# Moving the weight-sum transfers and the residual arithmetic of the MLP within a two-layer DiT kernel

## The chip, the cores and the metric

One core of one Trainium2 chip runs the whole program. The metric is the device time in microseconds (us) from the start to the end of one execution, lower being better. A measurement of this kernel can tell a change of about half a per cent.

## What is computed

The reference is a two-layer transformer block over 1024 latent tokens and 256 context tokens of width 1024, in fp32. Cut to what matters here:

```python
for l in range(2):                                       # need_ctx only for l == 0
    m_lat = silu(c) @ mod_w[l] + mod_b[l]                # shifts, scales, gates; m_ctx alike
    h  = modulate(xl, sh1, sc1)
    yl = mixer(h)      # l=0: Hyena long convolution + neighbourhood attention (natten)
                       # l=1: latent attention (MLA) + Fourier mixing
    xl = layer_norm(ALPHA * xl + g1 * yl)
    xl = layer_norm(ALPHA * xl + g2 * mlp(modulate(xl, sh2, sc2), mlp_w1[l], mlp_w2[l]))
    # the same two lines for xc where need_ctx
mlp(h, w1, w2) = square(relu(h @ w1)) @ w2               # 1024 -> 4096 -> 1024
```

## The kernel before, in words

Every fp32 product is made of three matrix products of rounded high and low parts (`mm3`, lines 168 to 170): ScalarE (ACT) makes the high part with a cast (L161), VectorE (DVE) the low part with a subtraction (L162), TensorE (PE) multiplies. The order of work on each engine is fixed when the program is built. DMAs are issued from two queues: SyncE (SP) issues the plain loads and stores, GpSimd (POOL) issues the others, and a queue that waits for one transfer's condition holds everything behind it. POOL also does small arithmetic: products of the convolution (L1030 to L1034, `sc`, `xc`), attention biases (L862, `n_g`), copies (`ob`), and reciprocal roots (L177, L194, L1838).

The stages, with their place in the profiled execution:

- **First stage** (0 to about 570 us, `first_stage`, L716): 24 blocks of input projections (`hyena_in`, `qkv_in`; raw weights `hwr`, split weights `hwh` and `hwl`, result `u`), woven with the spectra of the Hyena filters (`filter_spectra`; tiles `f_w`, `f_w3h`, `f_h`, `f_sdh`, `f_z`, `f_cf`, stored as `cfl`) and with modulation vectors (`modraw`, `modacc`).
- **Attention and convolution** of layer 0 (570 to 940 us, `attention_and_conv`): 80 jobs of neighbourhood attention, each with a row sum `acc`, woven with the long convolution.
- **Output projection** of layer 0 (940 to 1085 us, `mixer_out`).
- **MLP of layer 0** (`FastMlp`). The two products of the MLP are done with a seven-product scheme in place of eight (`PRODUCTS`, L1339). The first product is done in `pairs` (1085 to 1400 us): 16 pairs j, each with seven items; the partial sums for the first six (`EARLY`) were done ahead, during `mixer_out`, and their results wait in DRAM as `first` and `sums`. The item named `five` loads them back: `after5` (L1609) issues the loads of `m_e` from `first` (L1612) and `m_c` from `sums` (L1613) on SP behind the five-product, and then makes `m_f = m_y - m_e` (L1615), for which the next product's bank waits.
- **Context** (1400 to 1500 us, `context`, layer 0 only), then **passes** (1500 to 1910 us, `passes`, L1707): seven passes i = 0 to 6 over the hidden width, one product each, accumulating in 4 or 5 PSUM banks (m is the block of 128 rows). A bank is opened at i = 0, 2 and 4 (`OPENS`), and after the last item of a pass each bank is evicted (`evict`, L1761) by ACT or DVE into the 512-wide halves of the accumulators `m_ra` and `m_rb` (one for each half of the tokens). After i = 4 `close` and after i = 5 `base` (L1853, L1863) do the residual over the whole 1024 columns: `residual_sum` (L1818) loads the old x as `mres` on POOL (L1822), multiplies the accumulator by the gate (L1823), adds ALPHA times x (L1825); then come the statistics (`bn_stats`) and the normalisation (`norm`). `tail` (L1869) does this for the last 512 columns after i = 6.
- **Layer 1** repeats it: `MixerIn` and `mixer_cd_in` (1850 to 2065 us; `cx` loads, `c_pt` transposes, Fourier tables `d_csh` and `d_csl`), `mla` (2065 to 2480 us), `mixer_out`, pairs (2600 to 2720 and on), passes to 3237.5 us.

Small pieces of such vector work are queued in `self.side` and `self.late`, and each item of the MLP takes one or two from it (`aside(n)`, L1810).

Four of the right-hand factors of the second product (t1 to t4) are sums of blocks of `mlp_w2`. They are made by DMA alone: `weight_sums` (L1344) issues, per layer, 64 transfers of 512 KB on POOL into DRAM tiles `tsums`, plain copies and accumulating ones; and ahead of the four chains' first copies a 1x1 transfer (L1353) that reads a tile of the stage (`k.token`), to tie the transfers to the progress of the work. For each of eight tiles i the eight transfers follow one another, each on the result of the one before. Layer 0's are all taken in the first stage, four per block from block 5 on; layer 1's in `mla`, two per group of scores.

Of the kernel before, what the change touches and what calls it, by code (L numbers as in the profile page):

```python
# [10 lines left out]
F32 = mybir.dt.float32  # L11
F32R = mybir.dt.float32r
AF = mybir.ActivationFunctionType
ALU = mybir.AluOpType
# [213 lines left out]
def setup(k, es):  # L228
# [12 lines left out]
    k.silu = c.tile([128, KT, 2], F32, name="silu")  # L241
    k.co = {(s, t): c.tile([128, 2], F32, name=f"co{s}_{t}") for s in range(2) for t in range(NTT)}
# [438 lines left out]
def hyena_in(k, j, hw, up, pj):  # L681
# [4 lines left out]
    k.token = raw[0:1, 0, 0:1]  # L686
# [5 lines left out]
    for s, n in SPANS:  # L692
# [5 lines left out]
        else:  # L698
            nc.scalar.copy(u[:, L:], ps[:, :n])
    v = up.tile([128, T], F32, tag="uv", name="uv")  # L700
# [15 lines left out]
def first_stage(k, hp, er):  # L716
# [4 lines left out]
    with ExitStack() as es:  # L721
# [14 lines left out]
        sums = weight_sums(k, 0)  # L736
# [13 lines left out]
        for j in range(1, 24):  # L750
# [12 lines left out]
            for _ in range(4 if j > 4 else 0):  # L763
                next(sums, None)
# [22 lines left out]
def qkv_in(k, j, hw, up, pj):  # L787
# [7 lines left out]
    k.token = raw[0:1, 0, 0:1]  # L795
# [4 lines left out]
    for s, n in SPANS:  # L800
        yield
        ps = project(k, pj, wh, wl, s, n)
        nc.scalar.activation(out=u[:, s:s + n], in_=ps[:, :n], func=AF.Copy, scale=-0.125 if j < 4 else 1.0)
    yield
# [61 lines left out]
def natten(k, es, step):  # L866
# [89 lines left out]
    def attend(p, jobs):  # L956

        acc = sm.tile([128, 4, 2], F32, tag="acc", name="acc")[:, :len(jobs)]
        for ji, e in [(ji, e) for ji in range(len(jobs)) for e in range(2)]:
# [16 lines left out]
            lasts.append(vals)  # L976
            pend.append((p, e, job, ji, len(jobs), acc, pr))
# [366 lines left out]
def weight_sums(k, l):  # L1344

    w2 = k.mlp_w2[l].rearrange("(j t p) (d n) -> p j t d n", t=2, p=128, d=2)
    for i, dst in enumerate(k.tsums[l]):
        for to, term, add in ("t1", "b11", 0), ("t3", "b12", 0), ("t1", "b12", 1), ("t3", "b22", 1), ("t2", "t3", 0), ("t2", "b11", 1), ("t4", "t2", 0), ("t4", "b21", 1):  # L1350
# [3 lines left out]
            k.nc.gpsimd.dma_start(out=dst[:, RIGHT[to]], in_=src, accum_op=ALU.add if add else ALU.bypass)  # L1354
            yield True
# [32 lines left out]
class FastMlp:  # L1388
# [161 lines left out]
    def pairs(self):  # L1550

        k, nc, tt = self.k, self.k.nc, self.k.nc.vector.tensor_tensor
        new = lambda nm: self.out.tile([128, 512], F32, tag=nm, name="m_" + nm, bufs=2 if nm in "efgc" else 1)
# [6 lines left out]
        def item(p, make, bank, b, first, after):  # L1560
            def multiply(w):
                if first:
                    setattr(p, bank, self.bank(bank))
                self.product(getattr(p, bank), w, b, first)
# [9 lines left out]
        def pair(j):  # L1574
# [34 lines left out]
            def after5():  # L1609
                if early:  # L1610
                    p.e, p.c = new("e"), new("c")
                    nc.sync.dma_start(out=p.e, in_=k.first[j])  # L1612
                    nc.sync.dma_start(out=p.c, in_=k.sums[0, j // 2][:, j % 2])  # L1613
                p.f, p.g = new("f"), new("g")
# [901 lines left out]
```

## Time and profile before

| quantity | value |
|---|---|
| median of 3 runs | 3245.53 us (3235.15 to 3253.18) |
| the profiled execution's own time | 3239.32 us |
| its span, first to last instruction | 3237.5 us |
| TensorE busy (matmul) | 3055.5 us, 94% |
| VectorE, ScalarE, GpSimd busy | 2326.8, 1513.3, 534.6 us |
| mean granted TensorE clock | 0.977 |
| bytes moved by DMA | 557.82 MB, 172 GB/s |

The rows of the profile read as engine, tile names (written<-read) and line; a bracket at the end of a timeline row is the idle time of that engine just before the instruction, and what ended it. In rows by window there follow the window's length, each engine's busy time with its instructions in parentheses, the granted clock of TensorE, the share of the 16 DMA engines that were busy, and GB/s. In rows of waits: who waited, for whom, total us, times, longest. "SPq" is SyncE's issuing side. "PEld" is TensorE's loading of weights.

### The profile page before, as it was taken

What the parts mean: (1) busy time and instruction counts of PE and PEld (TensorE: products, weight loads), DVE (VectorE), ACT (ScalarE), POOL (GpSimd) and SP (SyncE); (2) the same over time, 40 slices, a digit from 0 to 9 for tenths busy, and PEclk for the clock granted to TensorE, in tenths of its full rate; (3) what the DMA queues carried; (4) which work ended last, traced back from release to release, by engine and by line L of the source; (5) the groups of instructions that cost most, each with busy time, mean ns of one, the idle gap of its engine ahead of it and who ended that gap; (6) DMA issues with size and microseconds to landing.
All of it is one profiled execution on the core that took longest, in us unless ns stands there. A gap on an engine that the chain in (4) does not pass through costs nothing. (4 is left out here: it accounts for less than half of the span.)

```text
span 3237.5 us, 46425 instructions
## 1 busy us (share of the span) xinstructions
PE 3055.5 (94%) x16500; PEld 2541.9 (79%) x16500; DVE 2326.8 (72%) x4456; ACT 1513.3 (47%) x3131; POOL 534.6 (17%) x800
## 2 busy tenths in 40 slices
PE   8898989899999899999999989999999999999997
PEld 4787878688877678888888777788888777888876
DVE  6566666788868876677675986688787887664577
ACT  3343333355553445555444445566665354554441
POOL 2202110222212121210000213112111212120000
PEclk9999999899999999999999999999999999999999
DMA  7648885433153464498785653255356355446564
GB/s 253 189 136 232 221 219 179 142 104 122 59 184 121 149 212 144 159 295 287 257 271 170 231 169 109 86 105 116 89 114 184 128 176 180 149 165 211 194 239 144
DMA packets 363557, 557.82 MB, mean 172 GB/s; under 512 B 33557, under 2 KB 226875, under 8 KB 362684
## 3 DMA queue, kind: packets, MB, share of 16 engines
q1 hardware_dynamic: 299484, 367.44, 35.2%
q0 software_dynamic: 63840, 187.41, 20.3%
q8 instruction: 130, 2.13, 0.3%
q14 instruction: 103, 0.84, 0.1%
HBM read 429.86 MB, written 193.65 MB: 193 GB/s over the span
## 5 line engine op out<-in xcount | busy, mean ns | idle before, releaser
L161 ACT CAST m_ph<-m_sl 128x512 fp32r<-128x512 f32 x216 | 134.1, 621 | 352.1 <-PE m_y L169 106.4
L162 DVE TENSOR_TENSOR m_pl<-m_sl,m_ph 128x512 fp32r<-128x512 f32 x216 | 148.5, 687 | 167.9 <-ACT m_ph L161 167.2
L161 ACT CAST m_ph<-m_w 128x512 fp32r<-128x512 f32 x224 | 135.9, 618 | 196.2 <-PE m_x L169 73.9
L315 DVE SCALAR_TENSOR_TENSOR modacc<-modraw,silu,modacc 128x512 f32<-128x512 f32 x224 | 162.5, 747 | 81.5 <-DMA modraw<-in_mod_w 80.6
L168 PE MATMUL pj<-hTh,hwh 128*128 128x512 f32 (+1 forms) x576 | 211.3, 368 | 1.4 <-ACT u L697 1.4
L169 PE MATMUL pj<-hTl,hwh 128*128 128x512 f32 (+1 forms) x576 | 209.2, 364 | 0.3 <-DVE hTl L219 0.3
L170 PE MATMUL pj<-hTh,hwl 128*128 128x512 f32 (+1 forms) x576 | 208.6, 362 | 0.3 <-DVE hwl L162 0.3
L162 DVE TENSOR_TENSOR m_pl<-m_w,m_ph 128x512 fp32r<-128x512 f32 x224 | 152.5, 683 | 9.8 <-ACT m_ph L161 9.4
L162 DVE TENSOR_TENSOR m_pl<-m_sr,m_ph 128x512 fp32r<-128x512 f32 x216 | 147.9, 685 | 6.7 <-ACT m_ph L161 4.6
L169 PE MATMUL m_x<-m_pl,m_ph 128*128 128x512 f32 x352 | 139.9, 398 | 6.1 <-DVE m_pl L162 6.1
L168 PE MATMUL m_x<-m_ph 128*128 128x512 f32 x352 | 131.6, 394 | 9.4 <-ACT m_ph L161 6.5
L170 PE MATMUL m_x<-m_ph,m_pl 128*128 128x512 f32 x352 | 138.8, 394 | 0.0
L161 ACT CAST m_ph<-m_sr 128x512 fp32r<-128x512 f32 x216 | 133.6, 619 | 9.1 <-PE m_x L169 5.9
L2341 ACT ACTIVATE a_p<-a_s,a_m 128x512 f32<-128x512 f32 (+1 forms) x192 | 116.3, 615 | 44.7 <-DVE a_m L2337 44.2
L1354 POOL DMA_DIRECT2D tsums<-in_mlp_w x96 | 96.8, 1021 | 220.6 <-DMA tsums<-tsums 108.2
L168 PEld LDWEIGHTS pj<-hTh,hwh 128*128 128x128 f32 x576 | 111.3, 194 | 18.6 <-ACT u L697 1.6
L169 PEld LDWEIGHTS pj<-hTl,hwh 128*128 128x128 f32 x576 | 111.6, 194 | 17.6 <-DVE hTl L219 1.6
L170 PEld LDWEIGHTS pj<-hTh,hwl 128*128 128x128 f32 x576 | 111.2, 193 | 17.2 <-DVE hwl L162 0.6
L2332 DVE TENSOR_REDUCE a_mx<-a_s 128x1 f32<-128x512 f32 (+1 forms) x192 | 110.9, 594 | 14.5 <-PE a_s L170 12.9
L168 PE MATMUL o_ps<-o_wh,yh 128*128 128x512 f32 x288 | 114.5, 400 | 2.1 <-ACT o_wh L161 2.1
L169 PE MATMUL o_ps<-o_wl,yh 128*128 128x512 f32 x288 | 114.3, 397 | 1.1 <-DVE o_wl L162 1.1
L170 PE MATMUL o_ps<-o_wh,yl 128*128 128x512 f32 x288 | 113.5, 395 | 0.0
(1319 smaller groups left out, 9928.8 us busy)
## 6 DMA issues: line engine op xcount, KB each, us to landing
m_sl<-sums SPq DMA_DIRECT2D x112, 512.0 KB
m_w<-in_mlp_w SPq DMA_DIRECT2D x108, 512.0 KB
tsums<-in_mlp_w POOLq DMA_DIRECT2D x96, 512.0 KB, 6.6
modraw<-in_mod_w SPq DMA_DIRECT2D x160, 256.0 KB
sums<-m_s POOLq DMA_DIRECT2D x128, 256.0 KB, 3.8
m_sr<-tsums SPq DMA_DIRECT2D x64, 512.0 KB
m_sr<-in_mlp_w SPq DMA_DIRECT2D x48, 512.0 KB
tsums<-tsums POOLq DMA_DIRECT2D x32, 512.0 KB, 4.0
```

The costliest lines, as they stand in the source:

```text
L161: nc.scalar.copy(hi, src)
L162: nc.vector.tensor_tensor(out=lo, in0=src, in1=hi, op=ALU.subtract)
L168: t.matmul(out, lh, rh, start=start, stop=False, skip_group_check=on)
L169: t.matmul(out, lh, rl, start=False, stop=False, skip_group_check=on)
L170: t.matmul(out, ll, rh, start=False, stop=stop, skip_group_check=on)
L315: k.nc.vector.scalar_tensor_tensor(out=acc, in0=w, scalar=c, in1=acc, op0=ALU.mult, op1=ALU.add)
L1354: k.nc.gpsimd.dma_start(out=dst[:, RIGHT[to]], in_=src, accum_op=ALU.add if add else ALU.bypass)
L2332: nc.vector.tensor_reduce(out=mx[:, i:i + 1], in_=ps[:, :n], axis=AX.X, op=ALU.min)
L2341: nc.scalar.activation(out=p_[:, s:s + n], in_=ss[i][:, :n], func=AF.Exp, bias=m, scale=-1.0, accum_out=acc[:, i:i + 1])
```

## The change

Four things are changed.

1. **Weight sums.** `weight_sums` goes through the eight terms outermost and the eight tiles innermost, so that a transfer's predecessor on the same tile lies eight transfers back. The 1x1 transfers are gone. In their place a POOL copy of one element (`k.after` from a token) stands before every transfer, and both are kept in program order. Layer 0: ACT copies one element of the block's result (`k.last`, a piece of `u`) into `k.tokens` in blocks 3 to 18, and two transfers follow in each of these blocks (32 in all); the other 32 are sent in attention, after jobs whose count leaves 1 or 3 modulo 5, with the job's `acc` as token. Layer 1: one transfer per score tile in `mla`, two per group as before.
2. **Early pairs.** The loads of `m_e` and `m_c` move from `after5` to `before5`, ahead of the five-product, and `m_e` has three buffers in place of two. Of the late sums, the last two change places.
3. **Passes.** The scaled input and the gate are applied to 512-wide partial sums: `base(m, half, h)` is queued after i = 1 (half 0, columns 0), i = 2 (half 1, columns 1) and i = 3 (the other two). What i = 4 and i = 5 bring is evicted as `q = ps * gate` (`gated`; 4 or 5 buffers `m_q`), and added to the accumulator later, with the statistics. `close` is then `end` and `norm`.
4. **Pacing.** The context takes a piece of side work at odd items alone; passes take one piece per item except in layer 0 outside i = 4 and outside odd items of i = 5, where they take two; the side work is emptied before the last item of i = 4.

The diff, cut:

```diff
+    for to, term, add in ("t1", "b11", 0), ("t3", "b12", 0), ("t1", "b12", 1), ("t3", "b22", 1), ("t2", "t3", 0), ("t2", "b11", 1), ("t4", "t2", 0), ("t4", "b21", 1):
+        for i, dst in enumerate(k.tsums[l]):
+            token = yield True
             src = dst[:, RIGHT[term]] if term in RIGHT else w2[...]
-            if not add and term not in RIGHT:
-                k.nc.gpsimd.dma_start(out=dst[0:1, RIGHT[to], 0, 0:1], in_=k.token)
-            k.nc.gpsimd.dma_start(out=dst[:, RIGHT[to]], in_=src, accum_op=ALU.add if add else ALU.bypass)
-            yield True
+            keep(nc.gpsimd.tensor_copy(k.after, token))
+            keep(nc.gpsimd.dma_start(out=dst[:, RIGHT[to]], in_=src, accum_op=ALU.add if add else ALU.bypass))
...
-            for _ in range(4 if j > 4 else 0):
-                next(sums, None)
+            if 2 < j < 19:
+                nc.scalar.copy(k.tokens[:, j:j + 1], k.last[0:1, 0:1])
+            for _ in range(2 if 2 < j < 19 else 0):
+                send(sums, k.tokens[:, j:j + 1])
...
+            if count[0] % 5 in (1, 3):
+                send(k.early_sums, acc[0:1, ji, e:e + 1])
...
-            def after5():
+            def before5():
                 if early:
                     p.e, p.c = new("e"), new("c")
                     nc.sync.dma_start(out=p.e, in_=k.first[j])
                     nc.sync.dma_start(out=p.c, in_=k.sums[0, j // 2][:, j % 2])
+
+            def after5():
                 p.f, p.g = new("f"), new("g")
                 tt(out=p.f, in0=p.y, in1=p.e, op=ALU.subtract)
...
+            elif i < 4:
+                tt(out=(b, a)[i - 2][:, hi], in0=ps, in1=b[:, lo], op=ALU.subtract)
             elif i < last:
-                d, x, y = ((b, ps, b[:, lo]), (a, ps, b[:, lo]), (a, a[:, hi], ps), (b, b[:, hi], ps))[i - 2]
-                tt(out=d[:, hi], in0=x, in1=y, op=ALU.subtract)
+                ends[m] = self.gated(self.tile_of(m, i - 4), (a, b)[i - 4], ps, hi, ALU.subtract, self.st[m, i - 4][:, 1])
+                next(ends[m])
...
+    def gated(self, t, a, ps, s, op, st):
+        tt = self.k.nc.vector.tensor_tensor
+        q = self.sm.tile([128, 512], F32, tag="q", name="m_q", bufs=5 if self.ctx else 4)
+        tt(out=q, in0=ps, in1=self.gate(t)[:, s], op=ALU.mult)
+        yield True
+        tt(out=a[:, s], in0=a[:, s], in1=q, op=op)
+        self.k.nc.vector.bn_stats(st, a[:, s])
+        yield True
...
-                self.aside(2)
+                self.aside(1 if not self.ctx or i == 4 or i == 5 and j % 2 else 2)
```

How the order of instructions moves on POOL, at three places. The first is the first stage, from the filter tables' loads on: `erp` and `rpx` are tables for the attention's biases, `tsums0_0` the sums' first tile. Before:

```order
L1353 DMA tsums0_0_233<-hwr_1805 1x1 x2
L1354 DMA tsums0_0_233<-in_mlp_w2 128x2x512 x4
L1354 DMA tsums0_0_233<-tsums0_0_233 128x1024
L666 DMA erp_256<-rp_zero_998 64x192
L667 DMA erp_256<-rp_zero_998 64x192
L1354 DMA tsums0_0_233<-in_mlp_w2 128x2x512
L671 DMA rpx_257<-erp_256 8x8x384 x16
```

The same place on POOL in the changed kernel:

```order
L668 DMA erp_258<-rp_zero_1000 64x192
L669 DMA erp_258<-rp_zero_1000 64x192
L673 DMA rpx_259<-erp_258 8x8x384 x16
L1361 COPY after_73<-tokens_74 1x1
L1362 DMA tsums0_0_235<-in_mlp_w2 128x2x512
```

The bias tables' transfers now stand ahead of every weight sum, and each weight sum has its copy of a token ahead of it.

The second place is attention on POOL, between two of the convolution's groups of products: `sc`, `xc` and `vc` are these products, `n_g0` a bias, `ob` an output of attention. Before:

```order
L1099 TENSOR_TENSOR vc_5630<-xc_5639 128x256
L862 TENSOR_TENSOR n_g0_5148<-n_g0_5148,rp_6545 128x256
L911 COPY ob_6128<-r_6126 128x512
L1030 TENSOR_TENSOR sc_6151<-xc_6152,cfc_5690 128x512
L1031 TENSOR_TENSOR xc_6152<-xc_6152,cfc_5690 128x512
```

The changed kernel has, from the same products on:

```order
L1105 TENSOR_TENSOR vc_5636<-xc_5645 128x256
L1106 TENSOR_TENSOR vc_5636<-xc_5645 128x256
L867 TENSOR_TENSOR n_g0_5150<-n_g0_5150,rp_6563 128x256
L1361 COPY after_73<-acc_5675 1x1
L1362 DMA tsums0_2_237<-tsums0_2_237 128x1024
```

Copies that wait for a job's `acc`, and transfers (this pair is the first of four that follow one another), now stand between the convolution's products; before, nothing of the sums was left in attention.

The third place is the boundary of the layers on POOL, where the last rows of layer 0 are stored (`xs1`) and layer 1's first work is prepared: `mres` is the old x, `cx` the new x read back. Before:

```order
L1822 DMA mres_18735<-xs0_6_129 128x1024
L1822 DMA mres_18753<-xs0_7_130 128x1024
L1822 DMA mres_18759<-xs0_9_132 128x1024
L2010 DMA cx_18865<-xs1_0_133 128x1024
L2010 DMA cx_19263<-xs1_1_134 128x1024
```

In the changed kernel all `mres` loads stand further ahead, `cx` follows its row's store at once, and the end of this part reads:

```order
L1864 DMA xs1_9_144<-m_rb4_13917 128x1024
L2108 DMA c_bdh_19784<-const_bdh 128x256
L2108 DMA c_bdl_19786<-const_bdl 128x256
L194 TENSOR_TENSOR co1_9_94<-co1_9_94,mhalf_65 128x1
L2199 DMA d_csh_19792<-const_csh 128x1024
L2260 COPY wqh_19736<-wqh_19736 128x3x8 x4
L2260 COPY wql_19737<-wql_19737 128x3x8 x4
L2199 DMA d_csl_19794<-const_csl 128x1024
L177 TENSOR_TENSOR rstd_19800<-rstd_19800,mhalf_65 128x1
```

The first loads of the Fourier tables `d_csh` and `d_csl` stood just ahead of the `mres` load of row 2 before; now they stand behind the last row's store, with reciprocal roots queued behind them.

More of the change, by code (lines that the diff above doesn't have):

```diff
@@ L699, in hyena_in @@
             nc.scalar.copy(u[:, L:], ps[:, :n])
+    k.last = u[:, L:]
     v = up.tile([128, T], F32, tag="uv", name="uv")
@@ L735, in first_stage @@
         extra = [(j, part) for j in range(2, 6) for part in range(2)]
-        sums = weight_sums(k, 0)
+        sums = k.early_sums = weight_sums(k, 0)
+        next(sums)
         steps = filter_spectra(k, tab, hid2, tneg, wk, ph, pz)
@@ L803, in qkv_in @@
         nc.scalar.activation(out=u[:, s:s + n], in_=ps[:, :n], func=AF.Copy, scale=-0.125 if j < 4 else 1.0)
+    k.last = u
     yield
@@ L1558, in store, with item @@
             nc.gpsimd.dma_start(out=k.sums[i, j // 2][:, j % 2], in_=a)
-        def item(p, make, bank, b, first, after):
+        def item(p, make, bank, b, first, after, before=lambda: None):
             def multiply(w):
@@ L1771, in run @@
             def run(*ops):
+                while i == 4 and j == nj - 1 and self.side:
+                    self.aside(1)
                 if i in OPENS and j == 0:
@@ L1816, in aside, with stats @@
                 self.side.pop(0)
-    def residual_sum(self, t, a):
-        nc = self.k.nc
-        x = self.xp.tile([128, D], F32, tag="mx", name="mres")
-        nc.gpsimd.dma_start(out=x, in_=self.src[t])
-        nc.vector.tensor_tensor(out=a, in0=a, in1=self.gate(t), op=ALU.mult)
-        yield True
-        nc.vector.scalar_tensor_tensor(out=a, in0=x, scalar=ALPHA, in1=a, op0=ALU.mult, op1=ALU.add)
-        yield True
-    def stats(self, m):
-        return self.sm.tile([128, 2, 6], F32, tag=f"st{m}", name="m_st")
+    def stats(self, m, half):
+        return self.sm.tile([128, 2, 6], F32, tag=f"st{m}{half}", name="m_st")
     def norm(self, t, a, st):
@@ L1851, in norm, with base, close @@
             yield True
-    def close(self, m, a):
-        t = self.tile_of(m, 0)
-        yield from self.residual_sum(t, a)
-        st = self.stats(m)
-        for h, s in enumerate(HALVES):
-            self.k.nc.vector.bn_stats(st[:, h], a[:, s])
-        yield True
-        yield from self.norm(t, a, st)
-    def base(self, m, a):
-        yield from self.residual_sum(self.tile_of(m, 1), a)
-        st = self.st[m] = self.stats(m)
-        self.k.nc.vector.bn_stats(st[:, 1], a[:, HALVES[1]])
+    def base(self, m, half, h):
+        nc = self.k.nc
+        t, s = self.tile_of(m, half), HALVES[h]
+        a = (self.ra, self.rb)[half][m][:, s]
+        x = self.xp.tile([128, D], F32, tag="mx", name="mres")[:, :512]
+        nc.gpsimd.dma_start(out=x, in_=self.src[t][:, s])
+        nc.vector.tensor_tensor(out=a, in0=a, in1=self.gate(t)[:, s], op=ALU.mult)
+        nc.vector.scalar_tensor_tensor(out=a, in0=x, scalar=ALPHA, in1=a, op0=ALU.mult, op1=ALU.add)
+        yield True
+        if half == h:
+            self.st[m, half] = self.stats(m, half)
+        if half == h == 0:
+            nc.vector.bn_stats(self.st[m, 0][:, 0], a)
+    def gated(self, t, a, ps, s, op, st):
[6 more added lines that the diff above has]
+        yield True
+    def close(self, m, end):
+        yield from end
+        yield from self.norm(self.tile_of(m, 0), self.ra[m], self.st[m, 0])
     def tail(self, m, ps):
-        a, s, tt = self.rb[m], HALVES[0], self.k.nc.vector.tensor_tensor
         while self.side:
@@ L1874, in tail @@
         t = self.tile_of(m, 1)
-        q = self.sm.tile([128, 512], F32, tag="q", name="m_q", bufs=2)
-        tt(out=q, in0=ps, in1=self.gate(t)[:, s], op=ALU.mult)
-        tt(out=a[:, s], in0=a[:, s], in1=q, op=ALU.add)
-        self.k.nc.vector.bn_stats(self.st[m][:, 0], a[:, s])
-        last = self.norm(t, a, self.st[m])
+        for _ in self.gated(t, self.rb[m], ps, HALVES[0], ALU.add, self.st[m, 1][:, 0]):
+            pass
+        last = self.norm(t, self.rb[m], self.st[m, 1])
         if self.then:
@@ L2390, in mla @@
         sums = weight_sums(k, 1)
+        next(sums)
         def advance():
@@ L2415, in mla @@
                     roped(g)
-                k.token = pr[0][1][0:1, 0:1]
-                for _ in range(2):
-                    next(sums, None)
+                for _, r in pr:
+                    send(sums, r[0:1, 0:1])
                 if g == 1 and h + 1 < NH:
```

30 lines of the change are left out of this document (19 added, 11 removed).

## The prediction

> **What bounds the kernel now.** I read the page's busy times and the granted clock first, then the busy times by stage, then the waits of TensorE and the timeline at its longest gaps.
>
> ```profile
> PE 3055.5 (94%) x16500; PEld 2541.9 (79%) x16500; DVE 2326.8 (72%) x4456; ACT 1513.3 (47%) x3131; POOL 534.6 (17%) x800
> core 0: 3237.5 us, clock 0.977
> ```
>
> TensorE is the bound: it is busy 3055.5 of 3237.5 us, so 182 us are idle. The clock is a second loss: a mean of 0.977 means that about 0.023 x 3237.5 = 74 us of full speed were not granted. The change adds no product and takes none away, so all that it can win lies in these 182 + 74 = 256 us. Where they lie, by stage (the columns after the length are PE, PEld, DVE, ACT, POOL, granted clock, DMA share, GB/s):
>
> ```profile
> 100.00:500.00 400.00, 363.22 (x2101) 318.73 (x2100) 255.57 (x500) 141.71 (x252) 76.23 (x98) 0.94 0.76 201
> 600.00:940.00 340.00, 325.03 (x2569) 274.14 (x2569) 273.48 (x587) 185.74 (x441) 65.77 (x74) 0.97 0.30 98
> 1050.00:1200.00 150.00, 132.46 (x541) 103.97 (x541) 114.17 (x183) 67.38 (x118) 32.47 (x58) 0.94 0.55 179
> 1200.00:1400.00 200.00, 199.77 (x895) 164.32 (x894) 132.28 (x205) 105.00 (x175) 38.55 (x72) 1.00 0.49 161
> 1400.00:1500.00 100.00, 93.53 (x755) 89.96 (x754) 82.77 (x175) 57.02 (x154) 15.96 (x19) 1.00 1.02 320
> 1500.00:1800.00 300.00, 300.00 (x1369) 247.14 (x1368) 197.58 (x368) 131.14 (x269) 4.37 (x7) 1.00 0.70 233
> 1800.00:2065.00 265.00, 241.38 (x1165) 204.27 (x1163) 207.54 (x502) 123.93 (x296) 67.78 (x96) 0.96 0.46 155
> 2065.00:2480.00 415.00, 396.44 (x2593) 343.69 (x2594) 323.86 (x713) 272.39 (x678) 76.28 (x136) 0.98 0.49 110
> 3100.00:3200.00 100.00, 87.50 (x368) 67.39 (x367) 84.20 (x130) 41.15 (x74) 7.12 (x10) 1.00 0.67 230
> ```
>
> In the middle of the pairs and of the passes (1200 to 1400, 1500 to 1800) TensorE is at 100% and full clock: work added to VectorE there, at 198 of 300 us, costs nothing. The losses sit at the seams and in the first stage. How an idle stretch turns into a second loss is seen just behind one, where the same products start at two spacings:
>
> ```profile
> 1149.06 0.63 PE L168 MATMUL m_y<-m_b221h,m_ph 128*128 128x512 f32 x1
> 1149.49 0.63 PE L169 MATMUL m_y<-m_b221l,m_ph 128*128 128x512 f32 x1
> ...
> 1152.46 0.39 PE L170 MATMUL m_y<-m_t10h,m_pl 128*128 128x512 f32 x1
> 1152.69 0.40 PE L168 MATMUL m_y<-m_t11h,m_ph 128*128 128x512 f32 x1
> ```
>
> 0.43 us from start to start, then 0.23: after a stall the products run at half speed for a while. Over the kernel 74 us of clock go with 182 us of idle time; by stage I add the stage's own clock loss to its idle time.
>
> **Weight sums in the first stage.** Idle time is 400 - 363.2 = 36.8 us, the clock another 0.06 x 400 = 24, together 61. Four stalls make 21.9 of the 36.8:
>
> ```profile
> 128.18 0.56 POOL L667 DMA_DIRECT2D erp<-rp_zero  x1
> 131.56 1.31 SPq L507 DMA_DIRECT2D f_w<-in_hy_w  x2
> 138.88 0.80 PE L525 MATMUL f_h<-f_w3h,f_hid 128*128 128x256 f32 x2 [7.53 <-ACT f_w3h L161]
> ...
> 163.14 0.42 ACT L516 ACTIVATE f_el<-f_el 128x256 f32<-128x256 f32 x1 [5.34 <-DMA f_el<-in_hy_log_decay]
> 165.59 0.45 PE L168 MATMUL f_z<-tab_fwch,f_sdh 128*128 128x128 f32 x1 [3.44 <-issue]
> ...
> 278.97 0.75 DVE L315 SCALAR_TENSOR_TENSOR modacc<-modraw,silu,modacc 128x512 f32<-128x512 f32 x1 [4.50 <-DMA modraw<-in_mod_w]
> 280.71 0.58 PE L526 MATMUL f_h<-f_w3l,f_hid 128*128 128x256 f32 x1 [5.04 <-DVE f_w3l L162]
> ...
> 403.51 0.69 DVE L586 TENSOR_TENSOR f_cf<-f_p,f_p 128x512 f32<-128x512 f32 x1 [5.29 <-DMA cfl<-f_cf]
> 411.06 0.58 PE L168 MATMUL f_z<-tab_fwlh,f_sdh 128*128 128x256 f32 x1 [5.90 <-ACT f_sdh L161]
> ```
>
> The first (7.53) starts on POOL: `erp` is issued behind weight sums, SP's order holds the `f_w` load until it is through, and the cast of `f_w` waits. In the changed order `erp` and `rpx` stand ahead of all sums, so I count this stall gone. The other three have a transfer of small size (`f_el`, `modraw`, `cfl`) ahead of them that is late or slow while the DMA engines are 76% busy. The sums' own rows say how crowded they are:
>
> ```profile
> L1354 POOL DMA_DIRECT2D tsums<-in_mlp_w x48: 702/1144/1282, 111.6 to 493.6; - x48
> ...
> tsums<-in_mlp_w POOLq DMA_DIRECT2D x48, 512.0 KB, 7.1
> ...
> L1354 POOL DMA_DIRECT2D tsums<-in_mlp_w x48: 707/1138/1213, 2098.2 to 2467.2; - x48
> ```
>
> Sixty-four transfers of 512 KB fall into this stage, and thirty-two are left: 16.8 MB of the stage's 80 (201 GB/s x 400 us) go, so a DMA share of 0.76 should become about 0.6. That shortens waits but doesn't end them, and the engines' own order stays. With 24/36.8 = 0.65 us of clock per idle us: first stall 7.5 x 1.65 = 12; a third of the other three, 14.4 x 1.65 / 3 = 8. **Term -20** (from 0, if other waits take their place, to -36, all four).
>
> The Trainium skill, on its page "DMA: Bandwidth & Descriptors" (section "Anatomy of one DMA — SWDGE (gpsimd) path"), fits a GpSimd transfer as 2.0 us and its bytes at 436 GB/s; for 512 KB this gives an estimate of 3.2 us against the 7.1 measured here. By that price an empty machine would win all four stalls and the term would be -36; no run here shows such a machine.
>
> **The other half, in attention.** Thirty-two copies and transfers join POOL between 600 and 940 us, where it is busy 65.8 of 340 us, TensorE 325 and VectorE 273. A transfer holds POOL for 1.1 us (row above). The copy isn't in the trace; POOL's nearest small rows are DMA issues of 0.56, so I take 0.6. That is 32 x 1.7 = 54 us, behind which the convolution's products queue:
>
> ```profile
> POOL sc L1030 <- DVE xc L1094: 58.0, 4, 34.2
> ```
>
> POOL waits long for VectorE's `xc` there, so most of it lies beside other waits. One tenth on the path: **term +5** (0 to +54). DMA share is 0.30 there and takes 16.8 MB without trouble. In `mla` the counts stay, 64 copies replacing 16 short transfers; POOL is 76 of 415 us busy: 0.
>
> The Trainium skill's "GPSIMD Engine Reference" (section "Specifications") says that GpSimd shares its SBUF interfaces with VectorE, and that they collide with VectorE instructions of two SBUF inputs; it speaks against moving POOL work to where VectorE is busiest. The trace doesn't bear it out for these instructions: a sum is issued in a median of 1144 ns where VectorE is 64% busy and 1138 ns in `mla` at 78%. By the rule the term would lie nearer its upper end.
>
> **Early pairs.** The next product waits for `m_f`, which waits for the `m_e` load, itself held on SP by a store of its buffer:
>
> ```profile
> PE m_y L168 <- DVE m_f L1615: 6.4, 3, 3.2
> ...
> SPq L1612 <- DMA sums<-m_e: 20.6, 4, 6.4
> ...
> PE m_y L168 <- DVE m_f L1615: 4.6, 3, 3.4
> ```
>
> The first two rows are of layer 0 (1050 to 1200 us), the last is of layer 1. With a third buffer the load has no longer to wait for that store, and it is issued one product earlier: 12 matmuls at 0.23 us, 2.8 us, beside waits of at most 3.4. Layer 0 loses 0.06 x 150 = 9 us of clock to 17.5 of idle time, 0.5 per us: 11.0 x 1.5 = 16.5. What is late next are the `m_pl` splits that already make the other 11 us idle there; I take three quarters. **Term -12** (0 to -17).
>
> **Boundary of the layers.**
>
> ```profile
> 1870.42 0.53 POOL L2010 DMA_DIRECT2D cx<-xs  x1 [2.33 <-DVE m_rb L1825]
> ...
> 1877.24 1.09 PE L2018 MATMUL c_pt<-ident,cx 128*128 128x128 f32 x4 [6.22 <-DVE cx L199]
> ...
> PE m_x L168 <- DVE m_rb L1766: 2.7, 1, 2.7
> ```
>
> Both are consequences of the 1024-wide residual, which is due all at once: `cx` is queued behind `mres` loads that wait for VectorE, and a bank is evicted behind residual work. In the change these loads and products are done two to three passes earlier, under a full TensorE. 8.9 us idle, and 0.04 x 265 = 10.6 of clock on 23.6 of idle time, 0.45 per us: 12.9. Not all: other `c_pt` and `c_ptk` waits stand behind. **Term -9** (+10, by the `d_csh` rival's first step below, to -13).
>
> **End of layer 1.**
>
> ```profile
> L1825 DVE SCALAR_TENSOR_TENSOR m_rb<-mres,m_rb 128x1024 f32<-128x1024 f32 x4 | 4.9, 1213 | 0.0
> L1877 DVE TENSOR_TENSOR m_rb<-m_rb,m_q 128x512 f32<-128x512 f32 x4 | 2.8, 692 | 0.1
> ```
>
> From 3100 to 3200 us TensorE is idle 12.5 us, VectorE busy 84. The residual there is 16 instructions of about 1.2 us (this row's kind, gate and x, for two halves of four blocks), 19.5 us; eight of 0.69 (the second row's kind) come in their place: 14 us leave VectorE. The last pass's `tail` is the same. A bit over half: **term -7.5** (0 to -12.5). **Context**: DMA share 1.02, idle 6.5 us; side work that loads `modraw` moves to the passes: **-2** (+2 to -4). The extra VectorE work in the passes (about 0.7 us per block and half) is covered by the stretch at 198 of 300 us; without that cover it would be 18 x 0.7 = 13 us.
>
> **Sum**: -20 + 5 - 12 - 9 - 7.5 - 2 = -45.5 us. Against the profiled execution's own 3239.3 us this is 3194 us. The median before is 3245.5, 6 us above it; this stays in the range. Half a per cent, which is about what a measurement here can tell, is 16 us.
>
> **Rivals.**
> *The first stage does not give.* Its other stalls have an engine as last releaser; if TensorE waits for VectorE's order and not for transfers, only the first stall goes: 12 in place of 20, and the freed time meets the next wait, so that the term is -8: 3206. For it speaks that the row at 280.71 names VectorE, against it the `modraw` wait 1.7 us earlier. Chance 0.15.
> *Gains are given back.* Attention takes +20 (a third of POOL's 54), the boundary +5 in place of -9, the first stage -10; with -12, -7.5, -2 it comes to -6.5: 3233, no change. Chance 0.16.
> *POOL holds the convolution, slower.* Each of the 32 copies waits for its own job's `acc`, and POOL is in order. 80 jobs take 340 us, 4.25 each. If a copy holds the convolution's products behind it for half a job, 2.1 us, and this reaches TensorE, 68 us come in place of 5: -50.5 + 68 = +17.5, 3257 us. It decides from 50.5/32 = 1.6 us per copy. For it: TensorE is busy 325 of 340 us with little slack, and VectorE is at 80%. Against it: POOL's 58 us of waiting for `xc`. Chance 0.11.
> Within the boundary's term there is a smaller one: `d_csh` and `d_csl` are now loaded behind the last `xs1` store, with reciprocal roots behind them.
>
> ```profile
> L2173 POOL DMA_DIRECT2D d_csh<-const_csh x8: 537/537/568, 1673.0 to 2052.9; - x8
> ...
> 1963.19 0.78 PE L168 MATMUL d_pf<-d_csh,c_abh 128*128 128x512 f32 x1
> ```
>
> Loaded at 1673.0 and first used at 1963.2; now there is little to spare, and a few us with a slow window after them, up to 10, are the term's upper end.
>
> **How the numbers follow.** Forecast 0.58 (faster), first rival 0.15 (faster by 33 us), second 0.16 (same), third 0.11 (over 0.5% slower). Of the forecast's cases few end within 16 us of before. Faster 0.72, same 0.17, slower 0.11. The terms' far ends together give 3239 - 82 = 3157; all at once are unlikely, so the range begins at 3160, and reaches to 3248, past the second rival and half of the way to the third; the third itself is left out.
>
> **What would show it.** Right: no stall over 5 us between 100 and 200 us on `f_h`; DMA share from 100 to 500 us near 0.6; no row of TensorE's waits for `m_f` over 1 us; `cx` at the boundary loaded before the last `mres`; VectorE from 3100 to 3200 us under 75 us. Wrong: TensorE from 600 to 940 us busy less than 315 us with `sc` or `xc` behind a wait of POOL for `acc`; or the same idle time in the first stage under other names.

## The result, and the profile after

| | before | changed |
|---|---|---|
| median | 3243.53 us (4 runs, 3235.15 to 3253.18) | 3160.22 us (4 runs, 3158.27 to 3164.11) |
| ratio | | 0.9744, 95% interval 0.9714 to 0.9774 |
| span of the profiled execution | 3237.5 us | 3156.5 us |

The change makes the kernel 83 us faster, 2.6%. The forecast was 45.5 us; the sign was right, the size a little over half, and the time lies at the lower end of the range. Two executions in the experiments below (10969 and 7559 us) are left out of all ratios and medians; the first was the profiled one of its kernel, which therefore has a time but no stages.

The page's busy times of the changed kernel, and its core's clock:

```profile
PE 3033.8 (96%) x16500; PEld 2530.3 (80%) x16500; DVE 2335.2 (74%) x4510; ACT 1515.7 (48%) x3147; POOL 548.7 (17%) x914
core 0: 3156.5 us, clock 0.983
```

The number of products is the same, so the 81 us of span come out of idle time and of clock, as the prediction had it: 182 us of TensorE's idle time became 122.7, and the clock's loss went from 74 us to 0.017 x 3156.5 = 54. Where the time went is best read from the places in the work at which each stage begins: the first or last product of a kind in either trace.

| stage (from one product to the next) | before, us | changed, us | difference | term forecast |
|---|---|---|---|---|
| start to first projection | 45.6 | 42.3 | -3.3 | |
| projections, first to last `pj` | 523.3 | 481.6 | -41.7 | -20 |
| attention, to first `o_ps` | 361.8 | 367.5 | +5.7 | +5 |
| output projection of layer 0 | 127.3 | 127.3 | 0.0 | |
| pairs of layer 0, to first `m_c` | 332.6 | 324.1 | -8.5 | -12 with layer 1 |
| context, `m_c` | 107.8 | 104.3 | -3.5 | -2 |
| passes of layer 0, to last `m_x` | 415.5 | 406.7 | -8.8 | -9 with the next |
| to the first score `a_s` of MLA | 175.3 | 174.6 | -0.7 | |
| MLA, to first `o_ps` of layer 1 | 388.8 | 383.3 | -5.5 | 0 |
| output projection of layer 1 | 138.5 | 139.1 | +0.6 | |
| pairs of layer 1 | 285.1 | 279.5 | -5.6 | above |
| passes of layer 1, to the last product | 327.6 | 314.9 | -12.7 | -7.5 |
| last product to the end | 8.3 | 11.3 | +3.0 | 0 |
| sum | 3237.5 | 3156.5 | -81.0 | -45.5 |

More than half of the gain is in the first stage. The stretches of the changed kernel that answer to those shown of before, by window (same columns):

```profile
100.00:500.00 400.00, 390.92 (x2363) 343.50 (x2362) 283.13 (x551) 160.58 (x288) 54.79 (x85) 0.99 0.62 179
530.00:890.00 360.00, 339.90 (x2610) 287.76 (x2610) 283.88 (x613) 182.20 (x444) 109.75 (x154) 0.93 0.54 151
1567.00:1690.00 123.00, 119.48 (x539) 98.61 (x538) 97.36 (x183) 48.12 (x100) 5.41 (x10) 0.97 0.82 276
1690.00:1854.00 164.00, 164.00 (x728) 135.61 (x727) 133.62 (x264) 77.89 (x161) 17.45 (x26) 1.00 0.61 209
3010.00:3123.00 113.00, 110.67 (x481) 89.26 (x480) 93.62 (x159) 50.11 (x90) 6.92 (x10) 1.00 0.66 233
```

From 100 to 500 us TensorE's idle time fell from 36.8 to 9.1 us and the clock is nearly full, with the DMA share at 0.62 where I expected about 0.6. What is left there of waits, in the changed kernel's waits of TensorE:

```profile
PE f_z L168 <- issue: 3.0, 1, 3.0
PE f_z L168 <- ACT f_sdh L161: 1.6, 2, 1.0
```

None of the four long stalls is left but the one at `f_z`, which went from 3.44 to 3.0 us. The row 1567 to 1690 is new ground that was not in the forecast: in these two passes of layer 0 TensorE was busy for the whole 115 us before, and now they hold a stall of 3.5 us (below). The 3.3 us at the start belong to no edit: the first projection comes at 42.3 to 45.6 us in all the kernels whose stages are read here.

### The profile page after: what moved, and what is told of

It reads as the page before. It is cut to its first block, busy times and chain, and to the rows that moved or that the text cites. A ratio compares the mean times of both kernels' runs of the same rounds, so it can differ in the third digit from the quotient of the medians.

```text
span 3156.5 us, 46710 instructions
## 1 busy us (share of the span) xinstructions
PE 3033.8 (96%) x16500; PEld 2530.3 (80%) x16500; DVE 2335.2 (74%) x4510; ACT 1515.7 (48%) x3147; POOL 548.7 (17%) x914
## 5 line engine op out<-in xcount | busy, mean ns | idle before, releaser
L2395 ACT CAST a_th<-a_ptr 128x512 fp32r<-128x512 f32 x160 | 90.9, 591 | 42.0 <-PE a_ptr L2392 40.2
```

The costliest lines, as they stand in the source:

```text
L2395: nc.scalar.copy(th, pt)
```

## The experiments

Each experiment's time is given as a ratio to runs of the kernel before on the same chip. "Stage" numbers are taken as in the table above, from one profiled execution, whose time lies up to 9 us from the median of its kernel; a difference of a few us in one stage is therefore compared with how much that stage varies among the kernels in which it was not touched.

**The sums alone, and all but the sums.** The first kernel is the one before with the edits to `weight_sums`, its tokens and its places; the second is the changed kernel without them.

```diff
-    for i, dst in enumerate(k.tsums[l]):
-        for to, term, add in ("t1", "b11", 0), ("t3", "b12", 0), ...:
+    for to, term, add in ("t1", "b11", 0), ("t3", "b12", 0), ...:
+        for i, dst in enumerate(k.tsums[l]):
...
+            keep(nc.gpsimd.tensor_copy(k.after, token))
...
-            for _ in range(4 if j > 4 else 0):
-                next(sums, None)
+            for _ in range(2 if 2 < j < 19 else 0):
+                send(sums, k.tokens[:, j:j + 1])
...
+            if count[0] % 5 in (1, 3):
+                send(k.early_sums, acc[0:1, ji, e:e + 1])
```

> The kernel before with the change of the weight sums alone (new order, tokens, half of layer 0's moved to attention); pairs, passes and pacing as before. If the parts add up, the projections end about 45 us earlier (569 to 524 us), attention takes 6 us longer, MLA about 5 us less: 3243 - 44 = 3199 us, ratio 0.986. If the parts need each other (the rival), it stays above 3215 us.

Measured: 0.9857 (0.9839 to 0.9875), 3194.7 us. Projections took 482.2 us, attention 361.5, MLA 383.7; every later stage of layer 0 and the end of layer 1 stood as before. The 6 us that attention was expected to lose did not appear.

> The changed kernel with the weight sums as they were before (64 in the first stage, chain by chain, short transfers as tokens). If the parts add up, the projections end at 569 us as before, and pairs, context, passes and the end of layer 1 give their 39 us: 3204 us, ratio 0.988. If most of the gain came through the sums, it stays above 3220 us.

Measured: 0.9876 (0.9856 to 0.9895), 3199.1 us. The two gains, 1.43% and 1.24%, sum to 2.67% against 2.56% for the whole: the parts add up, and the sums are somewhat more than half of it.

**What in the first stage.** Here stood the main question. Theory A: the load on the DMA engines makes the stalls. Theory B: POOL's order does, that is, `erp` behind the sums and the short transfers that read the raw weights' buffer. The changed kernel with all 64 of layer 0's sums in the first stage keeps the new order and the new tokens, and brings the load back:

```diff
-            for _ in range(2 if 2 < j < 19 else 0):
+            for _ in range(4 if 2 < j < 19 else 0):
...
-            if count[0] % 5 in (1, 3):
-                send(k.early_sums, acc[0:1, ji, e:e + 1])
```

> The changed kernel with all 64 of layer 0's sums in the first stage, four in each of the blocks 3 to 18, none in attention; order and tokens as changed. Theory A (the load on the DMA engines made the stalls): at least half of the 45 us comes back, the projections end at 545 us or later, total 3175 us or more. Theory B (POOL's order made them: short transfers that read the raw weights' buffer, bias tables behind the sums): the projections still end at 524 us within 6, attention is 6 us shorter, total about 3155 us.

Measured: 0.9865 (0.9847 to 0.9883), 3197.1 us. The products of the projections, before and in this kernel (duration min, median, max; first and last start):

```profile
L170 PE MATMUL pj<-hTh,hwl x576: 276/393/628, 45.6 to 568.9; 128*128 128x512 f32 x143, 128*128 128x256 f32 x49
```

```profile
L170 PE MATMUL pj<-hTh,hwl x576: 276/394/628, 44.1 to 569.2; 128*128 128x512 f32 x143, 128*128 128x256 f32 x49
```

523.3 us before and 525.1 here: the whole gain of the stage is gone, although no bias table stands behind a sum and no transfer reads the raw weights. Theory B falls. The stage's window and what waited in this kernel:

```profile
100.00:500.00 400.00, 362.43 (x2094) 315.11 (x2093) 253.94 (x497) 143.06 (x268) 86.22 (x146) 0.95 0.73 197
```

```profile
tsums<-in_mlp_w POOLq DMA_DIRECT2D x48, 512.0 KB, 13.3
```

```profile
DVE modacc L317 <- DMA modraw<-in_mod_w: 69.2, 26, 8.3
```

A sum now takes 13.3 us from issue to landing. In the kernel before, where each transfer waited for the one before it on the same tile, it took 7.1; the stage is as long all the same, so its length does not follow the time of one sum. VectorE waits 69.2 us for `modraw` (54.3 before); in the changed kernel the same wait is

```profile
DVE modacc L317 <- DMA modraw<-in_mod_w: 31.3, 26, 4.9
```

and with none of layer 0's sums in the stage (a run below) it is 16.8 us.

The long `f_h` stall at 138.9 us, which the prediction counted as gone by order, is indeed gone in this kernel, and it is worth nothing: the stage is as long as before, with more small stalls in its place.

**Bytes or number.** All 64 in the first stage, but each of half the columns; layer 0's MLP then reads a block of `w2` in place of the sums.

```diff
...
+            c = slice(0, 512 if l else 256)
+            keep(nc.gpsimd.dma_start(out=dst[:, RIGHT[to], :, c], in_=src[:, :, c], ...))
...
```

> All 64 of layer 0's sums in the first stage as in the run with all first, but each moves half the columns (256 KB); the passes of layer 0 read a block of w2 in place of the sums, so its MLP computes something else with the same traffic. If the bytes on the DMA engines make the stalls, the projections end at 524 us within 6, as with 32 full transfers, total about 3160 us. If the number of transfers and POOL's part (issue, tokens, queue) makes them, they end at 569 us, total about 3197 us.

Measured: 0.9759 (0.9734 to 0.9784), 3161.8 us. The projections:

```profile
L170 PE MATMUL pj<-hTh,hwl x576: 276/394/632, 43.7 to 532.5; 128*128 128x512 f32 x143, 128*128 128x256 f32 x49
```

488.8 us. With half the bytes and the same 64 copies and transfers, 36 of the 40 to 44 us are won; the number of transfers and POOL's part can be responsible for at most the other 4 to 8 (the eight profiled kernels with 32 full transfers lie between 481 and 485 us). The end at 532.5 us is 2.5 us outside what was expected of bytes alone, and 37 us from what was expected of the number.

**How much load.** Forty-eight in the first stage, and none:

```diff
-            for _ in range(2 if 2 < j < 19 else 0):
+            for _ in range(3 if 2 < j < 19 else 0):
...
-            if count[0] % 5 in (1, 3):
+            if count[0] % 5 == 1:
```

and, for the second,

```diff
-            for _ in range(2 if 2 < j < 19 else 0):
+            for _ in range(0):
...
-            if count[0] % 5 in (1, 3):
+            if count[0] % 5 != 4:
```

> The changed kernel with 48 of layer 0's sums in the first stage (three per block) and 16 in attention. If the cost goes in proportion to the bytes, the projections end half way between 524 and 569, at 546 us, total about 3180 us. If there is a threshold of load below which the stage hides them, they end below 535 us (threshold above 48) or above 558 us (below 48).

Measured: 0.9804 (0.9771 to 0.9838), 3175.6 us; projections

```profile
L170 PE MATMUL pj<-hTh,hwl x576: 276/394/632, 43.9 to 546.0; 128*128 128x512 f32 x143, 128*128 128x256 f32 x49
```

> The changed kernel with none of layer 0's sums in the first stage and 64 in attention, after four of five jobs. By the load theory the first stage has only 9 us of idle time and 4 of clock left to give: projections end at 513 to 522 us. If transfers are free in attention (362 to 368 us as with 0 and 32): total 3148 to 3158 us. Rival: 64 copies and transfers do hold the convolution: attention 375 us or longer, total 3165 us or more.

Measured: 0.9754 (0.9731 to 0.9778), 3159.1 us (the profiled execution 3166.0); projections

```profile
L170 PE MATMUL pj<-hTh,hwl x576: 276/394/632, 43.9 to 519.8; 128*128 128x512 f32 x143, 128*128 128x256 f32 x49
```

So the projections last 475.9 us with none, 481.6 with 32, 502.1 with 48 and 525.1 with 64. From 64 down to 32 each transfer costs 43.5/32 = 1.4 us, nearly in proportion, as was expected of the run with 48; below 32 there are 6 us left for all of them, 0.2 us each. Between none and 32 no run was made, so where exactly the line bends isn't known. The stage's window with none has a DMA share of

```profile
100.00:500.00 400.00, 395.54 (x2390) 347.30 (x2390) 289.79 (x563) 163.06 (x290) 12.50 (x21) 0.99 0.43 141
```

0.43, against 0.62 with 32, 0.68 with 48 and 0.73 with 64. In this stage load costs time from a mean share near 0.62 on, far from 1. That figure is a mean over 400 us and no limit of the engines, as a stretch of the kernel before shows in which the share is 0.86 and TensorE is busy for 98.8 of 100 us:

```profile
300.00:400.00 100.00, 98.80 (x600) 87.36 (x599) 65.15 (x120) 36.28 (x62) 18.18 (x22) 1.00 0.86 227
```

More sums in the stage also meant more of them sent one behind the other in each block (two, three or four); these runs don't separate the mean load from such bunches.

**What attention pays.** In the same kernel attention takes 379.5 us, 12 us longer than in the changed one: the gain in the first stage is spent again. The prediction's third rival names a mechanism for such a loss, POOL held at its tokens. POOL's wait there, in this kernel and then in the changed one:

```profile
POOL after L1361 <- ACT p L902: 139.9, 41, 10.5
```

```profile
POOL after L1361 <- ACT p L902: 138.9, 22, 22.0
```

Two waits of TensorE in this kernel:

```profile
PE pt L925 <- ACT th L926: 5.0, 1, 5.0
PE pr L942 <- POOL ob L916: 3.2, 2, 2.3
```

POOL stands at the tokens as long with 32 as with 64, so this wait does not tell the two kernels apart, and of TensorE's waits only 3.2 us name POOL (2.6 in the kernel with the sums alone, whose attention is short). There is a second candidate: from the last projection to the first `o_ps` the DMA share is 0.73 with 64 sums and 0.55 with 32, and 0.73 is the share at which the first stage lost 43.5 us. Which of the two costs the 12 us was not tested. To see what the changed kernel's 32 cost, they were left out; t2 and t4 are then not made, and the passes of layer 0 read t1 and t3 in their place.

```diff
-            if count[0] % 5 in (1, 3):
-                send(k.early_sums, acc[0:1, ji, e:e + 1])
...
-                    nc.sync.dma_start(out=b, in_=k.tsums[self.l][j // 2][:, RIGHT[r]])
+                    nc.sync.dma_start(out=b, in_=k.tsums[self.l][j // 2][:, RIGHT[r if self.l else {"t2": "t1", "t4": "t3"}.get(r, r)]])
```

> The changed kernel without the 32 sums that stand in attention: t2 and t4 of layer 0 are not made, and the passes read t1 and t3 in their place, so layer 0's MLP computes something else with the same traffic. If these 32 copies and transfers cost attention its 6 us: projections to the output projection take 362 us in place of 367.5, total 3154 us. If POOL doesn't hold the convolution and the 6 us come from elsewhere (the order of VectorE's and ScalarE's work): no change, 3160 us.

Measured: 0.9736 (0.9718 to 0.9754), 3158.8 us, not distinguishable from the changed kernel (its interval is 0.9714 to 0.9774). Attention took 365.5 us. Over all profiled kernels it took 361.5 to 368.8 us in the seven with 32 sums there (median 365.3) and 361.8 to 365.5 in the four with none (median 362.4). The 5.7 us of the table are within what this stage varies between builds; a cost of up to 3 us for 32 transfers is possible, but not shown.

**The MLP: pairs, pacing, residual.** The early pairs undone (loads behind the five-product, two buffers, old order of the late sums):

```diff
-            def before5():
+            def after5():
                 if early:
                     p.e, p.c = new("e"), new("c")
...
-                late.extend([lambda: sums(0), lambda: sums(1), lambda: sums(3), lambda: sums(2)])
+                late.extend([lambda: sums(0), lambda: sums(1), lambda: sums(2), lambda: sums(3)])
```

> The changed kernel with the early pairs as before (loads of m_e and m_c behind the five-product, two buffers for m_e, late sums in the old order). By the traces the pairs give 8.5 us in layer 0 and 5.6 in layer 1: total 3160 + 14 = 3174 us, with the waits of TensorE for m_f back at about 11 us. If the pairs' gain came from elsewhere (fewer transfers, the context's pacing), total 3164 us or less.

Measured: 0.9761 (0.9741 to 0.9781), 3164.8 us, and not the 3174 expected. By the total it can't be told from the changed kernel. By stages it can: pairs of layer 0 take 331.2 us (324.1 in the changed kernel) and of layer 1 283.9 (279.5), 11.5 us together, and the waits for `m_f` are back. Layer 0 is the firm part: 323 to 326 us in all ten profiled kernels with the early pairs, 331 to 333 in the three without. In layer 1 the output projection in front was 2 us shorter, which takes back part of the 4.4. First this kernel, layer 0, then the changed kernel, layer 0:

```profile
PE m_y L168 <- DVE m_f L1630: 7.2, 4, 3.7
```

```profile
PE m_y L168 <- DVE m_f L1633: 3.2, 2, 2.4
```

The changed kernel still has 3.2 us of this wait; the early load is not always early enough. SP's wait for the store of `m_e`, which the third buffer was to end (20.6 us in this window before), is still there:

```profile
SPq L1628 <- DMA sums<-m_e: 18.6, 3, 6.8
```

So it is mainly the earlier place of the load that helps; over the whole kernel SP's wait went from 43.5 to 33.1 us, TensorE's for this `m_f` from 11.0 to 4.3.

The pacing undone (a piece at every item of the context, two at every item of the passes):

```diff
-                if odd:
-                    self.aside(1)
+                self.aside(1)
...
-                self.aside(1 if not self.ctx or i == 4 or i == 5 and j % 2 else 2)
+                self.aside(2)
```

> The changed kernel with the pacing of before (a piece of side work at every item of the context, two at every item of the passes). If the new stall at the end of pass 2 of layer 0 (3.5 us and a half-speed window, 7.7 us on the second pair of passes) comes from modulation work pushed out of the context, it goes, and the context is 3 us longer: total 3156 us. If the pacing carries the gains at the end of the passes, total 3168 us or more.

Measured: 0.9799 (0.9776 to 0.9821), 3173.8 us: the pacing is worth some 14 us. The context is 3.2 us longer, and, as the second half of the expectation had it, more is lost at the end of the passes.

The complement has the pacing as changed, but the residual as it was before (the emptying of the side work before the last item of i = 4 goes with it):

```diff
-                ends[m] = self.gated(self.tile_of(m, i - 4), (a, b)[i - 4], ps, hi, ALU.subtract, self.st[m, i - 4][:, 1])
+                d, x, y = ((b, ps, b[:, lo]), (a, ps, b[:, lo]), (a, a[:, hi], ps), (b, b[:, hi], ps))[i - 2]
+                tt(out=d[:, hi], in0=x, in1=y, op=ALU.subtract)
...
+    def residual_sum(self, t, a):
```

> The changed kernel with the residual as before (whole 1024 columns after passes 4 and 5, no evictions through the gate) but with the new sums, pairs and pacing. Undoing the pacing alone cost about 14 us. If the residual in 512-wide pieces is what makes one piece of side work per item enough, this run loses more than that, since the old pieces are left over for the tail: 3180 us or more. If the pacing alone carries the gain at the end of layer 1, that end stays at 293 us from the first pass, and the run loses only the boundary of the layers: 3170 us or less.

Measured: 0.9771 (0.9751 to 0.9792), 3165.6 us. The third group of passes (i = 4 to 6) in layer 1 is where the prediction placed its end-of-layer term. Its window, from the group's first product to its last in order of items (the kept products of the end follow), in the kernel before, in the one without the pacing, and in the one with the pacing but the old residual, in this order (the changed kernel's row, 113 us, is above):

```profile
3081.00:3207.00 126.00, 113.50 (x482) 88.88 (x481) 100.24 (x156) 50.09 (x90) 7.12 (x10) 1.00 0.64 221
```

```profile
3017.00:3139.00 122.00, 113.61 (x483) 90.51 (x482) 94.44 (x160) 50.10 (x90) 6.98 (x10) 0.99 0.63 216
```

```profile
3019.00:3132.00 113.00, 110.30 (x480) 89.39 (x479) 92.89 (x148) 50.31 (x90) 6.09 (x9) 1.00 0.67 238
```

126, 122 and 113 us: with one piece of side work per item the old 1024-wide residual is as good there as the new one. What was in the way was two pieces at each item between the splits, not their sum. The residual matters in layer 0. Its third group of passes took 180 us before, 170 with the new residual and no pacing, 164 in the changed kernel, and with the old residual

```profile
1685.00:1864.00 179.00, 168.55 (x730) 137.44 (x729) 142.45 (x260) 78.86 (x163) 17.59 (x26) 0.97 0.60 208
```

```profile
1828.10 1.94 PE L2037 MATMUL c_pt<-ident,cx 128*128 128x128 f32 x8 [10.32 <-DVE cx L199]
```

179 us, with one stall of 10.3 us at `c_pt` that in the changed kernel is not there. The price of the new residual is the stall in the second group (i = 2 and 3), where its pieces now lie:

```profile
1629.14 0.77 PE L168 MATMUL m_y<-m_ph 128*128 128x512 f32 x1 [3.52 <-DVE m_rb L1784]
```

TensorE waits for the eviction of pass 2, in front of which VectorE has side work. The group takes 122.7 us; 115.0 before and 116.9 with the old residual. The size of this price varies: in the seven profiled kernels whose passes of layer 0 are those of the changed kernel the group takes 117.6 to 124.0 us and the stall 1.2 to 5.1, though their work there is the same (two of them load other blocks of the same size).

**Two tries to take that stall away.**

```diff
+                if not (self.ctx and i == 2 and j > nj - 4):
                     self.aside(1 if not self.ctx or i == 4 or i == 5 and j % 2 else 2)
```

> The changed kernel, in which the last three items of pass 2 of layer 0 take no side work. If side work in front of the evictions makes the new stall there, the second pair of passes takes 116 us in place of 122.7 and the total is 3154 us. If the modulation work is placed there by something else than these pieces, nothing changes: 3160 us.

Measured: 0.9746 (0.9727 to 0.9765), 3159.1 us; the second group took 120.1 us. Then with side work at every item of the context besides:

> The changed kernel with the context taking a piece of side work at every item, as before, and the last three items of pass 2 taking none; everything else as changed. If modulation work pushed out of the context is what crowds VectorE in the first four passes of layer 0, the second pair of passes takes 116 us (122.7 in the changed kernel) and the context 107.5 (104.3): total 3156 us. If the 512-wide residual pieces crowd them, the second pair stays at 120 us or more and the total is 3161 us.

Measured: 0.9756 (0.9737 to 0.9775), 3161.6 us; the second group took 119.9 us. Both figures, 120.1 and 119.9, lie inside the 117.6 to 124.0 of kernels without these edits, so the two tries show nothing, for either cause. The run without any pacing, which up to this group differs from the changed kernel in the context's pacing alone, took 115.8, below all of them; that speaks for the side work pushed out of the context, but it is one profile, and the run just shown speaks against it. What exactly crowds VectorE there stays open. No run beats the changed kernel by more than the measurement is uncertain.

## Why the prediction was right or wrong

- **Bound.** Idle time and clock at the seams, not work, was right: the same 16500 products take 81 us less of span.
- **First stage, forecast -20, measured -41.7.** The cause named, transfers that crowd the DMA engines, was right; the size failed in the term's own sum: "a third of the other three" stalls, and only four stalls counted. I reasoned from the DMA share that the waits would shorten in proportion (0.76 to about 0.6). The runs show a bend (a knee) instead: above 32 transfers each costs 1.4 us, below it 0.2 on the mean, and with 32 nearly all that can be had in this stage is had. Then the small idle pieces go as well (36.8 to 9.1 us), not just the named stalls. And the first stall, counted as gone by POOL's order, was worth nothing by itself: with the order changed and the load kept the stage was 525.1 us. The first rival, that the stage would give only 8 us, fell, and so did the second, that gains are given back: only the second group of passes in layer 0 gives back a few us. By the price on the Trainium skill's page "DMA: Bandwidth & Descriptors" (section "Anatomy of one DMA — SWDGE (gpsimd) path") I had put an empty machine, where a sum would land in an estimated 3.2 us, at -36. No run shows such a machine; the nearest, with no sums in the stage, measured 475.9 against 523.3 us, -47, more than the -36 by which I had priced my four stalls.
- **Attention, +5.** The difference in the table is +5.7, but that it fits is luck: without the 32 transfers it is as long within the variation between builds. 0 to 3 us fits these runs better at this dose. The third rival, 2.1 us for each of 32 copies, fell: 32 copies cost nothing like 68 us. At 64 attention does lose 12 us, but whether by this mechanism or by the load of the DMA engines is open. My 0.6 us for a copy was wrong too; in MLA one takes

```profile
L1361 POOL COPY after<-a_r x64: 173/173/328, 2034.2 to 2403.8; 1x1 f32<-1x1 f32 x64
```

  173 ns. The rule of the Trainium skill's "GPSIMD Engine Reference" (section "Specifications"), that GpSimd and VectorE collide at their SBUF interfaces, isn't borne out by 32 transfers in attention, where VectorE is busy for 271 of 340 us; whether any of the 12 us of the run with 64 is such a collision no run here tells.
- **Early pairs, -12, measured -8.5 and -5.6** by the table and 11.5 us lost by undoing them: right in size and in the wait for `m_f`, though it did not go entirely (3.2 and 1.2 us are left). One step was wrong: "With a third buffer the load has no longer to wait for that store". It still does, 18.6 us in layer 0 in place of 20.6.
- **Boundary, -9, measured -8.8 and -0.7.** The sum was right by two errors. The residual ahead of time gave more than I had counted in the third group (180 to 164 us), and took 7.7 us (2.6 to 9.0 in other builds) in the second group by a stall that I had excluded, since the extra VectorE work "is covered by the stretch at 198 of 300 us". The average over the stretch hides that work in front of an eviction has no cover. The smaller rival, the late load of `d_csh`, did not decide anything: from the last `m_x` to the first `a_s` it is 175.3 us before and 174.6 in the changed kernel. There is a stall of 4.4 us there,

```profile
1897.80 0.64 PE L2156 MATMUL c_ptq<-ident,cn 128*128 128x128 f32 x3 [4.37 <-DVE cn L2122]
```

```profile
DVE sw L2133 <- DMA c_rope<-const_ropet: 2.7, 1, 2.7
```

  but VectorE comes to it from a wait for another table, `c_rope`, and stalls of up to 3.2 us stood there before.
- **End of layer 1, -7.5, measured -12.7.** The step failed in its cause: "14 us leave VectorE". In the third group VectorE does 93.6 us of work in place of 100.2, and 92.9 with the old residual, so the 14 us did not leave it there. With the old residual and the new pacing the group is just as short (113 us); without the pacing it is 122. I had costed the pacing in a half sentence, for the context alone.
- **Context, -2, measured -3.5**: right. **MLA, 0, measured -5.5** and 5 us less in the kernel with the sums alone too, so it belongs to the sums there; by which wait, these runs don't tell. The 3 us more after the last product stay open as well.
- **The signs.** Three came: no `f_h` stall over 5 us, a DMA share of 0.62, and neither of the two signs of being wrong. Three did not: waits for `m_f` over 1 us are left, VectorE is busy for 93.6 of 113 us at the end of layer 1, as large a share as before and not under 75%, and no `cx` is loaded before the last `mres`; the `mres` loads are all done early (by 1713 us), and `cx` stands behind its row's store (first at 1757).
- **The range.** It held by 0.2 us, and that is luck. It began at 3160 because the far ends of all terms were thought unlikely together; the first stage (-41.7 against -36) and the end of layer 1 (-12.7 against -12.5) went beyond theirs, and MLA's 5.5 us were not in the sum at all.

## What to carry to other kernels

Load on the DMA engines can cost time well below a mean share of 1: find the bend by moving a quarter, half and all of the movable bytes out of a stage, and expect more than the named stalls to go when you are past it. Count what the stage that takes the bytes then pays. When one part of a change gives time, try the order and the load apart; a stall that an order removes may come back elsewhere while the load stands. Pacing of side work (how many pieces at each step) deserves its own line in the sum: at the end of layer 1 it was worth more than the work that was moved out. And before a stage's few us are read as an effect, see how much the stage varies among builds that don't touch it; here that undid two experiments.

## What the runs showed of the hardware that I had not expected

The same work in the first stage took 43.5 us longer at a mean DMA share of 0.73 than at 0.62, and only 6 us longer at 0.62 than at 0.43. That is 1.4 us for each further transfer of 512 KB. With four of them sent one behind the other in place of two, one takes 13.3 us to land in place of 7.7:

```profile
tsums<-in_mlp_w POOLq DMA_DIRECT2D x32, 512.0 KB, 7.7
```

This last row is the changed kernel's. A GpSimd copy of one element takes 0.17 us in attention and in MLA (medians) and 0.45 us in the first stage, so tying a transfer to a place in the work costs little so long as the token is ready.
